# The order of the down projection's loads: from the planner's choice to program order, with two granules in other tiles

## The chip, the cores and the metric

The kernel runs on one core of a Trainium2 chip. The metric is the device time of one execution in microseconds; a profile is one further execution with the hardware profiler, with its own time beside its span. TensorE (PE) multiplies, VectorE (DVE), ScalarE (ACT) and GpSimd (POOL) work on tiles in SBUF, and transfers between DRAM and SBUF are issued here by SyncE (SP, plain loads and stores) and by POOL (among others the transfers that add into their target).

## The reference, cut to what matters

One layer of an encoder block is computed for two request groups of 256 and 512 tokens with the same weights, 768 tokens together: three token mixers side by side, a gated merge with an output projection and a residual, and then the feed-forward part, which ends in the product that this change touches:

```
D_MODEL = 1024
D_FF = 2816                      # -(-8 * D_MODEL // (3 * 256)) * 256

x = x + merged @ w_out[li]
h2 = rmsnorm(x, ffn_norm_g[li])
g, up = jnp.split(h2 @ w_gate_up[li], 2, axis=-1)
x = x + (jax.nn.silu(g) * up) @ w_down[li]      # (768 x 2816) @ (2816 x 1024)
```

Everything is float32. The two row groups of x are the outputs.

## The kernel before, in words

**Precision.** A float32 product is made of three matmuls on a high and a low part of each operand (`mm3`, lines 751 to 753). The parts come from a split: ACT rounds the operand into the high part (line 742 for weights, called `whd`, line 745 for hidden values, `dxh`), and DVE subtracts that from the operand (`wld`, line 743, and `dxl`, line 746).

**Gate and up.** The hidden dimension is worked through in 11 blocks `fb` of 256 columns, each a gate product and an up product (`block`). Each block's result stands in a tile `fa` (two in rotation, of 2 x 768 floats in each of 128 partitions) and is stored to DRAM as `hid_scr[fb]` by `hid_store` on SP (line 1425). The last steps of a block are products on POOL (line 1422). A block also uses two staging tiles of the pool `stg` (tag `brr`, 768 floats, two in rotation) for its sums; nothing uses them after the last block.

**Down.** The product of the hidden values (768 x 2816) with `w_down` (2816 x 1024) is cut into halves in all three dimensions and done with seven products in place of eight, in the order P2, P1, P5, P6, P3, P7, P4. The summed dimension is 2 x 1408, and each half is walked in six granules `g`: five of 256 and one of 128, the last being half of block 10. So there are 42 items (product, granule). An item multiplies a hidden granule (384 tokens) with a weight granule (512 columns): 3 token tiles x 2 slices x 3 matmuls = 18 matmuls with 512 columns, 9 for a half granule.

The hidden granules `da{r}{kh}_{g}` (r is the half of the tokens, kh that of the summed dimension) are loaded from `hid_scr` by `a_load` (line 1719), 384 KB each, 192 KB for the half one, 24 in all. P2 needs the six with (r, kh) = (0, 1), P1 the six with (0, 0), P5 the twelve with r = 1; the later products use sums of what is there. Granules 0 to 3 of P2 (blocks 5 to 8) have a pool of their own, `dae`. The other 20 have one tile each in the pool `downa`.

The weights come as quarters of 512 KB (256 KB for the half granule) by `w_fetch`: `dwr` tiles (P2, P3) into the weight stream's three raw buffers, `dwt` tiles (P7) into three buffers, and six `dch` tiles, which P1 loads (line 1737). P5, P6 and P4 each add another quarter to `dch` by an accumulating transfer from POOL (line 1747), after the tile's last split; P7 loads a `dwt` (line 1745) and adds a quarter to it likewise. `make` splits an item's weight and its hidden granule (or a sum of granules, line 1760). `item_loads` issues the hidden loads that an item is the first to need.

**Staging.** The main loop runs over the items; at item i it asks for the hidden loads of item i + 7 and the weights of item i + 6, splits item i + 2, and multiplies item i. Ahead of it, inside the last up block (`down_early`, a hook after that block's first product), the weights of items 0 to 2 and the hidden granules 0 to 3 of P2 are loaded and items 0 and 1 split. After the block, its store, and the closing of the pools of the feed-forward part, follow the hidden loads of items 4 to 6 and the weights of items 3 to 5. The high and low weight parts have four tiles each, the hidden parts three each. At the end of P1, P3, P7 and P4 the results are added to `x1` (line 1834) and stored (line 1836).

**Memory.** Pools lie on a stack. The pools of the down stage are opened after `XB` (the normalised input in two parts, 49,152 bytes in a partition) and the feed-forward pools behind it (first the two `fa` tiles, 12,288 bytes, then scratch, sums and factors) have been closed, and take their place from the same address: first `downa` (20 x 3,072 = 61,440 bytes, exactly XB and both fa tiles), then `dch` (six of 4,096), then the small ones.

**Order.** What each engine and each queue does is a fixed order, made when the program is built by a planner that follows a simulated timeline: of what is ready in its model it takes one after the other, so the order on SP, ACT or POOL need not be that of the program text. Waits keep it correct on the chip: an instruction waits for the data, and for the buffer, that it needs, and what stands behind it on its engine waits too. A call `tc.keep_in_program_order(ins)` adds an edge from the instruction traced last on the same engine to `ins`: it is queued behind it, without waiting for it to finish.

Of the kernel before, what the change touches and what calls it, by code (L numbers as in the profile page):

```python
# [8 lines left out]
F32 = mybir.dt.float32  # L9
# [617 lines left out]
def hybrid_block(ctx, tc, A, outs, consts):  # L627
    nc = tc.nc
    v, act, gp, pe = nc.vector, nc.scalar, nc.gpsimd, nc.tensor
    mul, add, sub = ALU.mult, ALU.add, ALU.subtract  # L630
# [200 lines left out]
    hid_scr = [dr.tile([128, 2, TOK], F32, name=f"hid_scr{fb}") for fb in range(NFB)]  # L831
# [139 lines left out]
    with tc.tile_pool(name="nrm", bufs=1) as pool, tc.tile_pool(name="nrmg", bufs=1) as pg:  # L971
# [43 lines left out]
        g = bcast_load(pg, A["norm_mix_g"][0], 1024, "gmix")  # L1015
# [107 lines left out]
    stg = x1ctx.enter_context(tc.tile_pool(name="stg", bufs=2))  # L1123
# [12 lines left out]
    for i, nme in enumerate(("diff_q_g", "diff_k_g")):  # L1136
        g = rp[:, 2, 64 * i : 64 * i + 64]
# [247 lines left out]
    with tc.tile_pool(name="gelu", bufs=1) as yp:  # L1385
        for m in range(2):
            gelu_load(m, yp)
        for j, h in enumerate(DIFF_HEADS):
# [3 lines left out]
            for n_v, u_ in enumerate(v_units(last // 2) if h is None else qk_units(h)):  # L1392
                n_unit += 1
                W.by_dma = n_unit >= LOADED and not final
                m, r = divmod(n_unit, GELU_UNITS)
# [4 lines left out]
                if final and n_v % 2:  # L1400

                    t = slice(128 * (n_v - 1), 128 * (n_v + 1))
# [8 lines left out]
    HT = TOK // 2  # L1411
# [68 lines left out]
    with ExitStack() as c5:  # L1480
# [66 lines left out]
        for c in range(4):  # L1547
            w = W.get()
            for m in range(2):
                M = 2 * c + m  # L1550
                t = gtp.tile([128, TOK], F32, name=uid("gt"), tag="glr")
# [151 lines left out]
    ITEMS = [(p, g) for p in range(7) for g in range(NG)]  # L1703
    AHEAD, FETCH, LOAD = 2, 6, 7
    EARLY = 4
    NEW = {P2: ((0, 1),), P1: ((0, 0),), P5: ((1, 0), (1, 1))}
    de = ctx.enter_context(ExitStack())
    de.enter_context(tc.tile_pool(name="dgap", bufs=1, side="right")).tile([128, 16], F32, name="dgap")
# [2 lines left out]
    DP, a_raw, ch, w_raw, parts = {}, {}, {}, {}, {}  # L1711

    def a_load(q, g):

        r, kh = q
        fb, m, n = granule(kh, g)
        early = q == (0, 1) and g < EARLY
        t = (da_e if early else DP["a"]).tile([128, 2, HT], F32, name=f"da{r}{kh}_{g}")[:, 0:n]
        nc.sync.dma_start(t, hid_scr[fb][:, m : m + n, HT * r : HT * r + HT])
        a_raw[q, g] = t  # L1720

    def w_quarter(kh, f, g):
        fb, m, n = granule(kh, g)
        return wd[:, 2 * fb + m : 2 * fb + m + n, 512 * f : 512 * f + 512]

    def w_fetch(i):

        if i >= len(ITEMS):
            return
        p, g = ITEMS[i]  # L1730
        n = granule(0, g)[2]
        view = lambda t: t.rearrange("p (k c) -> p k c", k=2)[:, 0:n]
        acc = None
        if p in (P1, P5, P6, P4):
            if p == P1:
                ch[g] = view(DP["ch"].tile([128, 1024], F32, name=f"dch{g}"))
                nc.sync.dma_start(ch[g], w_quarter(0, 0, g))
            else:
                acc = {P5: (0, 1), P6: (1, 1), P4: (1, 0)}[p]
            t = ch[g]  # L1740
        else:
            t = view(DP["r"].tile([128, 1024], F32, name=f"dwt{i}", tag="dwt") if p == P7 else
                     W.praw.tile([128, W.HALF], F32, name=f"dwr{i}", tag="wr"))
            src, acc = {P3: ((1, 1), None), P7: ((0, 1), (1, 1)), P2: ((1, 0), None)}[p]
            nc.sync.dma_start(t, w_quarter(*src, g))
        if acc:
            gp.dma_start(t, w_quarter(*acc, g), accum_op=add)
        w_raw[i] = t

    def make(i):  # L1750
# [39 lines left out]
    def down_early():  # L1790
        for i in range(3):
            w_fetch(i)
        for i in range(EARLY):
            item_loads(i)
        for i in range(AHEAD):
            make(i)

    for what, fb in order[2:]:
        block(what, fb, down_early if (what, fb) == order[-1] else None)
# [5 lines left out]
    with ExitStack() as c7:  # L1805
        for k, n in (("a", 1), ("ch", 1), ("t", 2), ("r", 3)):
            DP[k] = c7.enter_context(tc.tile_pool(name="down" + k, bufs=n))
        HOME = {P1: (0, 0, add), P5: (1, 1, add), P6: (0, 1, sub), P3: (0, 1, add), P7: (1, 1, sub),
                P2: (0, 0, add), P4: (1, 0, add)}
        acc = {}  # L1810
        for i in range(EARLY, LOAD):
            item_loads(i)
        for i in range(3, FETCH):
            w_fetch(i)
        for i, (p, g) in enumerate(ITEMS):
            item_loads(i + LOAD)
            w_fetch(i + FETCH)
            make(i + AHEAD)
            bank = "b" if p in (P1, P6, P7, P4) else "d"
            if g == 0 and p in (P1, P5, P2):  # L1820
                acc[bank] = [PS[bank].tile([128, 512], F32, name=uid("dn"), tag=bank) for _ in range(3)]
            ps = acc[bank]
            n = granule(0, g)[2]
            xh, xl, wh, wl = parts.pop(i)
            for t in range(3):
                c = slice(128 * t, 128 * t + 128)
                for k in range(n):
                    mm3(ps[t], xh[:, k, c], xl[:, k, c], wh[:, k], wl[:, k],
                        g == 0 and k == 0 and p in (P1, P5, P2), g == NG - 1 and k == n - 1, p in (P6, P3, P7, P4))
            if g == NG - 1:  # L1830
                r, f, op = HOME[p]
                for t in range(3):
                    o = x1[3 * r + t][:, 512 * f : 512 * f + 512]
                    v.tensor_tensor(out=o, in0=o, in1=ps[t], op=op)
                    if p in (P1, P3, P7, P4):
                        nc.sync.dma_start(os_[3 * r + t][:, 512 * f : 512 * f + 512], o)
# [45 lines left out]
```

## Time and profile before

| | us |
|---|---|
| time, median of 3 runs | 1786.07 (1783.4 to 1786.67) |
| the profiled execution's own time | 1785.03 |
| its span | 1783.3 |
| PE busy | 1746.8 (98%) |
| DVE busy | 1263.0 (71%) |
| ACT busy | 887.1 (50%) |
| POOL busy | 280.2 (16%) |
| first matmul of the down projection, from the start of the span | 1601.8 |
| start of its last matmul | 1778.8 |

The profile's page gives busy times and 40 slices of the span, with the clock that was granted to TensorE and the load on the DMA engines. A query of the trace narrows this to a stretch, a tile or an engine. An engine's instruction is written as line, engine, operation and "output <- inputs" by the names in the program, with tile numbers left out; "SPq" is the issue of a transfer, which lands later. In brackets, or behind a bar, stands the idle time ahead of it with what ended it.

### The profile page before, as it was taken

The page shows a single profiled execution, that of the slowest core. Times are in us where ns is not written, and L with a number is a line of the kernel's source. Part 1 is how long each engine was busy: PE and PEld are TensorE (multiplying, and loading weights), DVE is VectorE, ACT ScalarE, POOL GpSimd, SP SyncE. Part 2 cuts the span into 40 slices and gives each one's busy share as a digit, 9 for nine tenths or more (in the row PEclk, how much of TensorE's full clock was granted, in tenths as well). Part 3 has the DMA queues.
Part 4 walks back from the last instruction along what each step waited for, and adds up shares of the span by engine and source line. Part 5 has one row for each costly group of instructions (what it writes and reads, how often), then busy time and mean ns, then how long its engine had stood idle before and what let it go on. Part 6 is the DMA issues. An engine that isn't in the chain of part 4 may idle for free.

```text
span 1783.3 us, 29404 instructions
## 1 busy us (share of the span) xinstructions
PE 1746.8 (98%) x11194; PEld 1612.8 (90%) x11194; DVE 1263.0 (71%) x2342; ACT 887.1 (50%) x1856; POOL 280.2 (16%) x300
## 2 busy tenths in 40 slices
PE   9999999999999999999999999999999999997999
PEld 8999988999999999999978888888899999996787
DVE  6765659699999589778865535442797768764774
ACT  6445434777676356777755434232343334333343
POOL 0000000000000101110110002000136555532210
PEclk9999999999999999999999999999999999998999
DMA  7223745654656466453872437322223232349852
GB/s 255 82 84 97 141 112 127 165 144 132 154 144 153 125 160 157 113 113 78 179 174 78 135 116 248 115 93 83 71 78 107 89 115 98 125 144 320 163 115 67
DMA packets 209661, 234.09 MB, mean 131 GB/s; under 512 B 57832, under 2 KB 173296, under 8 KB 209520
## 3 DMA queue, kind: packets, MB, share of 16 engines
q1 hardware_dynamic: 184080, 164.05, 30.4%
q0 software_dynamic: 24288, 65.02, 17.1%
q10 hardware_dynamic: 1152, 3.15, 0.5%
q8 instruction: 88, 1.44, 0.3%
q14 instruction: 53, 0.43, 0.1%
HBM read 165.78 MB, written 41.22 MB: 116 GB/s over the span
## 4 chain that ended last, share of the span: by engine, by line
PE 56%; DMA 5%; DVE 1%; issue 1%; ACT 0%; POOL 0%; SPq 0%; DVEq 0%; ACTq 0%; POOLq 0%
PE br L752 4%; PE br L751 4%; PE br L753 4%; PE gate L751 3%; PE gate L752 3%; PE gate L753 3%; PE up L752 3%; PE up L751 3%; PE up L753 3%; DMA da<-hid_scr 2%; PE dn L753 2%; PE dn L752 2%; PE dn L751 2%; PE av L1311 2%; PE qk L752 2%; PE qk L751 2%
## 5 line engine op out<-in xcount | busy, mean ns | idle before, releaser
L595 ACT ACTIVATE wh<-wr 128x1024 fp32r<-128x1024 f32 x124 | 140.5, 1133 | 74.5 <-PE br L752 30.8
L601 DVE TENSOR_TENSOR wl<-wr,wh 128x1024 fp32r<-128x1024 f32 x82 | 108.3, 1323 | 84.8 <-ACT wh L595 83.0
L751 PE MATMUL gl<-Hhi,wh 128*128 128x256 f32 (+1 forms) x384 | 132.4, 345 | 2.3 <-ACT glt L1114 2.3
L753 PE MATMUL gl<-Hhi,wl 128*128 128x256 f32 (+1 forms) x384 | 129.0, 336 | 0.0
L752 PE MATMUL gl<-Hlo,wh 128*128 128x256 f32 (+1 forms) x384 | 128.7, 335 | 0.0
L751 PE MATMUL qk<-wh,Hhi 128*128 128x256 f32 x384 | 108.7, 283 | 0.6 <-ACT V L1210 0.6
L752 PE MATMUL qk<-wl,Hhi 128*128 128x256 f32 x384 | 109.3, 285 | 0.0
L753 PE MATMUL qk<-wh,Hlo 128*128 128x256 f32 x384 | 108.5, 282 | 0.0
L599 POOL DMA_DIRECT2D wl<-wr x42 | 36.6, 872 | 452.9 <-ACT wl L598 439.5
L751 PE MATMUL dn<-whd,dxh 128*128 128x512 f32 x231 | 91.8, 398 | 10.9 <-ACT dxh L745 10.9
L753 PE MATMUL dn<-whd,dxl 128*128 128x512 f32 x231 | 89.8, 398 | 3.6 <-DVE dxl L746 3.6
L752 PE MATMUL dn<-wld,dxh 128*128 128x512 f32 x231 | 91.6, 397 | 0.0
L751 PEld LDWEIGHTS gl<-Hhi,wh 128*128 128x128 f32 x384 | 72.3, 188 | 9.7 <-ACT glt L1114 2.7
L753 PEld LDWEIGHTS gl<-Hhi,wl 128*128 128x128 f32 x384 | 72.0, 188 | 8.0
L752 PEld LDWEIGHTS gl<-Hlo,wh 128*128 128x128 f32 x384 | 72.2, 188 | 7.2
L1280 DVE TENSOR_REDUCE nm<-sc 128x1 f32<-128x512 f32 (+1 forms) x96 | 56.6, 597 | 26.5 <-PE sc L1275 25.4
L751 PEld LDWEIGHTS qk<-wh,Hhi 128*128 128x128 f32 x384 | 73.1, 190 | 1.5 <-ACT V L1210 0.8
L753 PEld LDWEIGHTS qk<-wh,Hlo 128*128 128x128 f32 x384 | 73.4, 191 | 0.3
L752 PEld LDWEIGHTS qk<-wl,Hhi 128*128 128x128 f32 x384 | 73.1, 190 | 0.6
L745 ACT ACTIVATE dxh<-da 128x768 fp32r<-128x768 f32 (+1 forms) x36 | 28.5, 791 | 87.5 <-PE dn L752 58.3
L557 ACT ACTIVATE wh_S<-ws 128x512 fp32r<-128x512 f32 x70 | 41.2, 625 | 61.2 <-PE up L752 33.9
L558 DVE TENSOR_TENSOR wl_S<-ws,wh_S 128x512 fp32r<-128x512 f32 x70 | 58.4, 858 | 14.8 <-ACT wh_S L557 14.8
(478 smaller groups left out, 6039.4 us busy)
## 6 DMA issues: line engine op xcount, KB each, us to landing
wr<-in_w_in_dram SPq DMA_DIRECT2D x48, 512.0 KB, 4.8
wr<-in_w_gate_up_dram SPq DMA_DIRECT2D x44, 512.0 KB, 3.5
wl<-wr POOLq DMA_DIRECT2D x42, 512.0 KB, 5.2
wr<-in_w_branch_dram SPq DMA_DIRECT2D x24, 512.0 KB, 4.1
glr<-gl_scr POOLq DMA_DIRECT2D x24, 384.0 KB, 3.5
hid_scr<-fa SPq DMA_DIRECT2D x11, 768.0 KB, 6.4
wr<-in_w_mem_kv_dram SPq DMA_DIRECT2D x16, 512.0 KB, 3.7
wr<-in_w_in_dram SPq DMA_DIRECT2D x32, 256.0 KB, 4.3
```

Source lines behind the costliest of these rows:

```text
L557: self.nc.scalar.activation(f(hi), src, AF.Copy)
L558: self.nc.vector.tensor_tensor(out=f(lo), in0=src, in1=f(hi).bitcast(F32), op=ALU.subtract)
L595: self.nc.scalar.activation(hi, r, AF.Copy)
L599: self.nc.gpsimd.dma_start(lo, r.bitcast(F32R), accum_op=ALU.add)
L601: self.sub.tensor_tensor(out=lo, in0=r, in1=hi.bitcast(F32), op=ALU.subtract)
L745: act.activation(hi, src, AF.Copy, scale=scale)
L751: pe.matmul(ps, wh, xh, start=start, stop=False, **kw)
L752: pe.matmul(ps, wh, xl, start=False, stop=False, **kw)
L753: pe.matmul(ps, wl, xh, start=False, stop=stop, **kw)
L1280: v.tensor_reduce(out=nm[:, m : m + 1], in_=ps, axis=AX.X, op=ALU.max, negate=True)
L1311: pe.matmul(po[:, 0:128], aT[:, 128 * k : 128 * k + 128], V[:, c0 // 128 + k, 128 * (h % 2) : 128 * (h % 2) + 128], start=(k == 0), stop=( ...
```

## The change

All loads of hidden granules, all loads of down weights and all accumulating transfers are passed through `pin`, which is `tc.keep_in_program_order`. Granules 4 and 5 of the first product P2, so far the first two tiles of `downa`, go into the two staging tiles `brr`, and `downa` holds 18 tiles (55,296 bytes) in place of 20; the pools behind it begin 6,144 bytes lower. The weight loads of items 3 and 4 are asked for inside `down_early`, one behind each of its two splits, and so in the program text ahead of the last block's store; they were asked for after it. Item 5's stays where it was. The output stores and the hidden stores are not pinned, but a pinned load is queued behind those that stand ahead of it in the text.

```diff
@@
+    pin = tc.keep_in_program_order
@@ a_load
-        early = q == (0, 1) and g < EARLY
-        t = (da_e if early else DP["a"]).tile([128, 2, HT], F32, name=f"da{r}{kh}_{g}")[:, 0:n]
-        nc.sync.dma_start(t, hid_scr[fb][:, m : m + n, HT * r : HT * r + HT])
-        a_raw[q, g] = t
+        name = f"da{r}{kh}_{g}"
+        if q == (0, 1):
+            t = da_e.tile([128, 2, HT], F32, name=name) if g < 4 else \
+                stg.tile([128, 2, HT], F32, name=name, tag="brr")
+        else:
+            t = DP["a"].tile([128, 2, HT], F32, name=name)
+        a_raw[q, g] = t[:, 0:n]
+        pin(nc.sync.dma_start(t[:, 0:n], hid_scr[fb][:, m : m + n, HT * r : HT * r + HT]))
@@ w_fetch
-                nc.sync.dma_start(ch[g], w_quarter(0, 0, g))
+                pin(nc.sync.dma_start(ch[g], w_quarter(0, 0, g)))
...
-            nc.sync.dma_start(t, w_quarter(*src, g))
+            pin(nc.sync.dma_start(t, w_quarter(*src, g)))
         if acc:
-            gp.dma_start(t, w_quarter(*acc, g), accum_op=add)
+            pin(gp.dma_start(t, w_quarter(*acc, g), accum_op=add))
@@ down_early
         for i in range(AHEAD):
             make(i)
+            w_fetch(i + 3)
@@
-        for i in range(3, FETCH):
+        for i in range(AHEAD + 3, FETCH):
             w_fetch(i)
```

## The prediction

> **What bounds the kernel now.** I began with the page: where TensorE stops, and at what clock it goes on.
>
> ```profile
> span 1783.3 us, 29404 instructions
> PEclk9999999999999999999999999999999999998999
> ```
>
> A slice is 44.6 us; the one dip of the granted clock is the 37th, 1605 to 1650, inside the down projection, which is the stretch that the diff touches. The next view is a table of stages for the instructions of its accumulator tile alone, then the same tile's list with first and last start, then what PE waited for.
>
> ```profile
> 1601.80:1618.30 16.50, 16.48 (x72) 13.36 (x72) 0.00 (x0) 1.00 1.05 375
> 1618.30:1629.20 10.90, 0.05 (x1) 0.00 (x1) 0.00 (x0) 0.60 1.11 253
> 1629.20:1634.30 5.10, 5.10 (x13) 3.99 (x14) 0.00 (x0) 0.53 1.10 248
> 1634.30:1658.60 24.30, 24.30 (x108) 19.89 (x106) 1.96 (x3) 1.00 1.09 312
> 1662.40:1668.20 5.80, 5.80 (x14) 4.54 (x15) 0.68 (x1) 0.50 0.42 70
> 1668.20:1779.20 111.00, 110.94 (x490) 91.51 (x488) 10.92 (x17) 1.00 0.50 106
> ```
>
> ```profile
> L751 PE MATMUL dn<-whd,dxh x231: 387/389/792, 1601.8 to 1778.3; 128*128 128x512 f32 x116
> L753 PE MATMUL dn<-whd,dxl x231: 388/389/792, 1602.3 to 1778.8; 128*128 128x512 f32 x116
> ```
>
> ```profile
> PE dn L751 <- ACT dxh L745: 10.9, 1, 10.9
> PE dn L753 <- DVE dxl L746: 3.6, 1, 3.6
> ```
>
> In a stage row the first pair is PE's busy time and count, and the last three figures are the granted clock, the DMA share and GB/s. PE stops twice, 10.9 and 3.6 us, and after each stop runs some 13 matmuls at half clock (0.53, 0.50). At full clock a matmul takes 110.94 / 490 = 0.2264 us. From the first start to the last (1778.8 - 1601.8 = 177.0 us) lie 692 steps of the 693 matmuls (three forms of 231), which need 156.7 us. **So 20.3 us are lost here**: 14.5 in the two waits, 5.10 - 13 x 0.2264 = 2.2 and 5.80 - 14 x 0.2264 = 2.6 in the slow clock behind them, the other 1.0 at the modelled edges. The 490 matmuls from 1668 on have no hole.
>
> What PE waited for are splits of hidden granules, and these waited for loads. The SP queue in order of time, then three pieces of the chain that ended last:
>
> ```profile
> 1591.71 4.53 SPq L1745 DMA_DIRECT2D dwr<-in_w_down_dram  x2
> 1597.86 2.99 SPq L1737 DMA_DIRECT2D dch<-in_w_down_dram  x6
> 1600.88 0.53 SPq L1745 DMA_DIRECT2D dwt<-in_w_down_dram  x1
> 1601.51 0.49 SPq L1745 DMA_DIRECT2D dwr<-in_w_down_dram  x1
> 1602.34 1.69 SPq L1745 DMA_DIRECT2D dwt<-in_w_down_dram  x2
> 1605.05 0.34 SPq L1425 DMA_DIRECT2D hid_scr<-fa  x1
> 1606.40 5.97 SPq L1745 DMA_DIRECT2D dwr<-in_w_down_dram  x3
> 1615.07 30.11 SPq L1719 DMA_DIRECT2D da<-hid_scr  x20
> ```
>
> ```profile
> 1605.05 9.94 DMA hid_scr<-fa
> 1616.94 20.02 DMA da<-hid_scr
> 1644.85 16.33 DMA da<-hid_scr
> ```
>
> Product P2, the first, uses six dwr tiles, and P7, the sixth, the dwt tiles. So three dwt loads (P7) and the three dwr loads at 1606.40 (the seventh to ninth, of P3, the fifth product) went out ahead of the hidden granules that P2 and P1, the next products, still lacked. All 20 of those sit in a pool over the memory of XB and of the two fa tiles (20 x 3,072 = 49,152 + 12,288 bytes), and the first was issued at 1615.07, when the last fa tile's store had landed (1605.05 + 9.94). They then joined a queue that was already full: 20.0 and 16.3 us to landing.
>
> **The change, part by part.** With no stall, a full granule (18 matmuls) takes 4.08 us and the half one 2.04; P2 starts at 1601.8, its items 4 and 5 at 1618.1 and 1622.2, P1 at 1624.2, P5 at 1646.6, and the last pair of P5 at 1667.0.
>
> *Right granules 0 to 3 of P2 move behind three weight loads.* They were issued one by one, the first at 1466.9; pinned, they follow the third dwr load, and the first two dwr loads follow the store of block 9.
>
> ```profile
> L1719 SPq DMA_DIRECT2D da<-hid_scr x24: 326/544/5322, 1466.9 to 1644.8; - x24
> 1574.73 1.79 SPq L1745 DMA_DIRECT2D dwr<-in_w_down_dram  x2
> 1576.98 0.34 SPq L1425 DMA_DIRECT2D hid_scr<-fa  x1
> 1587.38 4.70 SPq L1745 DMA_DIRECT2D dwr<-in_w_down_dram  x2
> da<-hid_scr SPq DMA_DIRECT2D x1, 384.0 KB, 3.4
> 1580.00:1600.00 20.00, 20.00 (x117) 20.00 (x116) 12.24 (x20) 7.34 (x11) 3.55 (x3) 1.00 0.41 136
> L745 ACT ACTIVATE dxh<-da 128x768 fp32r<-128x768 f32 x27 | 22.8, 844 | 63.2 <-PE dn L752 48.7 <-DMA da<-hid_scr 12.1 <-PE dn L753 2.4
> L746 DVE SCALAR_TENSOR_TENSOR dxl<-da,dxh 128x768 fp32r<-128x768 f32 x27 | 25.7, 953 | 26.7 <-ACT dxh L745 26.7
> ```
>
> The two dwr loads lose under 3 us, and splitting them begins later anyway (the slots for halves come free as PE leaves the block). The four loads (4 x 0.54 us of SP) go out at about 1587.8 to 1590. Alone one takes 3.4 us; with the dwr load 2.1 MB are under way, 5.8 us at 0.36 MB/us, so they land between 1591.5 and 1594. Three granules are then split inside the last block, at 0.84 us of ACT and 0.95 of DVE each, 2.5 and 2.9 us; cover is there (ACT 7.3, DVE 12.2 of 20 us busy), and the first is needed at 1601.8. Cost: 0; without the cover, at most these 5.4 us.
>
> *The fourth and fifth dwr load move ahead of the last store in the program text.* Their buffers, and so their times (1591.71 and 1595.9), stay as they are. 0.
>
> *The store is alone.* Nothing is left on SP between 1596.3 and the store. Its last product on POOL ends at 1603.72, so it starts 1.3 us sooner, and with only granule 4's load beside it (now in a staging tile, free with that same product) takes between the 4.6 us of one alone and the 9.94 of this one; I take 6.5, nearer the lower, as the queue is empty. It lands at 1610.3 (1608.4 to 1613.7).
>
> ```profile
> 1601.72 2.00 POOL L1422 TENSOR_TENSOR fa<-fa,fs 128x384 f32<-128x384 f32 x2 [1.62 <-DVE fs L1458]
> hid_scr<-fa SPq DMA_DIRECT2D x1, 768.0 KB, 4.6
> da<-hid_scr SPq DMA_DIRECT2D x4, 384.0 KB, 18.7
> dch<-in_w_down_dram POOLq DMA_DIRECT2D x1, 512.0 KB, 15.8
> L742 ACT ACTIVATE whd<-dch 128x1024 fp32r<-128x1024 f32 x20 | 20.9, 1045 | 6.1 <-PE dn L753 6.1
> L743 DVE TENSOR_TENSOR wld<-dch,whd 128x1024 fp32r<-128x1024 f32 x20 | 24.4, 1219 | 6.3 <-ACT whd L742 6.3
> ```
>
> *Everything else of SP queues behind granule 5, which waits for that store.* This is the added wait: behind it stand P2's last dwr (256 KB) and, in turn, a hidden granule and a dch tile for each item of P1, none of which needs the store, and which before were half there (dch out at 1597.86). Rates: plain loads moved 375 GB/s before the stall, the mixes 248 to 312; I count 0.36 and, as a bound, 0.25 MB/us. From 1610.3, up to the first dch go 0.20 + 0.39 + 0.26 + 0.39 + 0.52 = 1.77 MB, 4.9 to 7.1 us and 2.3 to land (3.4 us of the load alone less its 1.1 at that rate): 1617.5 to 1620. P1's first split must begin 2.3 us (1.05 + 1.22) ahead of 1624.2, at 1621.9. Each further item brings 0.92 MB, 2.5 to 3.7 us of 4.08. Granule 4 lands by 1610, 8 us early, granule 5 and the last dwr by 1615, 7 us early. Cost: 0; each us by which the store is later than 1613 would show in PE from here on.
>
> *P5's pairs.* After P1's 5.5 MB (done by 1626 to 1632) come six pairs of hidden granules, 4.3 MB, and beside them on POOL six accumulating transfers, 2.9 MB, that start as before when P1's weights are split. 7.2 MB take 23 us at 0.31 and 29 at 0.25: 1649 to 1661. The last pair is needed 3 us ahead of 1667.0, at 1664. Cost: 0, with a margin of 3 us at the bound.
>
> *Loads and transfers that move later.* P3's dwr loads go behind P1's output stores (1649), 40 us early for a product that starts near 1691. P7's first three dwt go behind P3's last dwr, that is behind the split of P3's third weight.
>
> ```profile
> 1704.19 9.96 SPq L1745 DMA_DIRECT2D dwr<-in_w_down_dram  x3
> dwt<-in_w_down_dram POOLq DMA_DIRECT2D x1, 512.0 KB, 7.5
> 1740.78 0.90 POOL L1747 DMA_DIRECT2D dwt<-in_w_down_dram  x1 [3.36 <-DVE wld L743]
> ```
>
> The last of those three went out at 1713.8, 2 us after P3's start (1779.1 - 3 x 22.4 = 1711.9). So the first dwt goes out 2.5 us into P3, lands 3.7 later, and its sum (7.5) is there at 14 us of P3's 22.4; it is split near 20. P4's transfers now stand on POOL behind P7's last, which goes out 6.5 us into P7 (1740.8 against 1779.1 - 2 x 22.4 = 1734.3): the first lands at 15 and is split at 20. Cost 0, margins 5 to 6 us. Removed with them: 4.7 MB (three dwr, three dwt and their sums) from the queue of 1601 to 1629.
>
> **The sum**: -20.3 us, nothing set against it. The profiled execution took 1785.03 us, 1.7 over its span, and the median of the three runs is 1786.07. 1785.0 - 20.3 = 1764.7; on the median, **1765.8, which I round to 1766**.
>
> **The rivals.** *A, the first wait stays in part.* ACT works in a fixed order, and in the old one it converts a hidden granule behind weights of later items. If granule 4's conversion stands behind the first or second split of P1's dch (1617 to 1620) it ends 3 us after 1618.1, plus 2.4 for the clock: **1771**. Against it: granule 4 no longer lands after them, so the planner has no reason for that order.
>
> *B, the second wait stays.* POOL's transfers do not wait their turn with SP: a dch sum issued at 1617 took 15.8 us beside hidden loads that took 18.7. If SP gets half of 0.36 MB/us as long as sums run (from 1619.5), its 9.8 MB less 3.3 end at 1656; with half of the 0.31 of the mixes, at 1662; a little less, and the old 3.6 + 2.6 us are back: **1772**. The Trainium skill, DMA: Bandwidth & Descriptors, section Queues, rings and completion order, states that each DMA engine goes round-robin between the queue rows that have work, a packet at a time; by that rule program order on SP gives its loads no precedence over POOL's, and the time would be B's 1772 rather than 1766.
>
> *C, slower: the wait for the store starves SP.* Between 1615 and 1661 SP's 7.1 MB moved at only 0.15 MB/us. If its 9.8 MB behind the store run no faster, the last pair lands at 1610 + 65 = 1675, 12 us late, and with two cold clocks (4.8) most is given back: **1783**. It decides below 0.135 (73 us, 19 us late, +24 with the clock): **1790**. Against it: in those 46 us 5 to 6 MB of other traffic ran beside SP, now 2.9.
>
> *D, the planner's new order undoes it.* Pins also move what ACT and DVE do in between; both partial waits together would leave **1778**.
>
> **How the numbers follow.** Full recovery 0.56, A 0.15, B 0.13, D 0.05, C 0.11 (0.03 of it within 0.2%, 0.08 slower). 0.2%, 3.6 us, is about what a measurement of this kernel tells from no change. Faster 0.88, same 0.04, slower 0.08. The range for 8 in 10 takes in full recovery, A and B with some play: 1763 to 1776.
>
> **What would show it.** Right: one row of hidden loads after the store without dwt or early dwr between; landings of 4 to 10 us instead of 13 to 20; no PE wait over 1 us between 1601 and the end and no row under clock 1.00; last matmul near 1758.5. Wrong: ACT waiting on a dwr or dch load ahead of granule 4 (A); DVE's subtraction on a load after 1645 (B); SP idle past 1613 for the store (C); P2 starting later than 1602 (the moved granules).

## The result, and the profile after

| | before | after |
|---|---|---|
| median of 5 runs each | 1786.07 us (1783.4 to 1787.73) | 1779.35 us (1776.34 to 1780.47) |
| ratio, 95% interval | | 0.9962 (0.9948 to 0.9977) |
| profiled execution, span | 1785.03, 1783.3 us | 1780.2, 1778.4 us |
| down projection, first matmul's start to the last one's end | 1601.82 to 1779.14: 177.32 us | 1606.17 to 1774.30: 168.13 us |

The change makes the kernel faster by 4.1 to 9.3 us (0.23% to 0.52% of 1786), 6.7 in the medians. The prediction said 20 us, and the time lies above its range. In the two profiled executions the stage is 9.2 us shorter, of which 4.4 are missing from the whole because the stage started later; what that is comes below.

The same table of stages as before, for the instructions of the accumulator tile alone, of the kernel after. The columns are PE's busy time (matmuls), weight loads, DVE, then the granted clock, the DMA share and GB/s.

```profile
1606.18:1641.28 35.10, 35.10 (x154) 28.72 (x154) 2.04 (x3) 1.00 0.89 267
1641.28:1644.63 3.35, 0.01 (x1) 0.00 (x0) 0.00 (x0) 1.00 1.06 390
1644.63:1645.13 0.50, 0.49 (x1) 0.19 (x1) 0.00 (x0) 0.91 1.10 384
1645.13:1647.07 1.94, 0.00 (x1) 0.01 (x1) 0.00 (x0) 0.50 1.06 373
1647.07:1652.20 5.13, 5.13 (x13) 4.08 (x14) 0.00 (x0) 0.53 1.10 290
...
1749.54:1751.59 2.05, 0.00 (x0) 0.03 (x1) 0.68 (x1) 1.00 1.13 206
```

And what PE waited for in that stage, in us, times, and the longest:

```profile
PE dn L752 <- DVE wld L743: 3.3, 1, 3.3
PE dn L751 <- DVE x L1840: 2.0, 1, 2.0
PE dn L753 <- DVE dxl L746: 1.9, 1, 1.9
```

The wait of 10.85 us inside P2, ahead of its fifth granule, is gone: 154 matmuls, P2 and half of P1, run in one piece at full clock. But two new waits stand in P1, 35 us into the stage, 3.35 and 1.94 us; the clock falls in between, and 13 matmuls then take 5.13 us instead of 2.94, 2.2 us too many. A third, of 2.05 us, stands at the start of P4, the last product. With the one slow matmul between the first two (0.3) that is 9.8 us; the stage is 10.85 longer than the 157.28 us that it takes without a hole (shown below), and the remaining 1.0 us is spread over the edges of these stretches.

The SP queue, in order of time:

```profile
1596.07 6.24 SPq L1750 DMA_DIRECT2D dwr<-in_w_down_dram  x2
1607.60 0.53 SPq L1725 DMA_DIRECT2D da<-hid_scr  x1
1609.55 0.34 SPq L1425 DMA_DIRECT2D hid_scr<-fa  x1
1613.21 0.96 SPq L1725 DMA_DIRECT2D da<-hid_scr  x2
...
1624.46 1.90 SPq L1725 DMA_DIRECT2D da<-hid_scr  x2
```

The pins did what they say: granule 4, the store, then granule 5 and everything else in program order, and no weight of P3 or P7 in between. The two loads at 1624.46 are the first pair of P5. The second of them, issued at 1625.83, landed at 1642.39, 16.6 us later. DVE, in order:

```profile
1631.93 0.95 DVE L746 SCALAR_TENSOR_TENSOR dxl<-da,dxh 128x768 fp32r<-128x768 f32 x1
1642.48 0.96 DVE L1765 TENSOR_TENSOR da<-da,da 128x768 f32<-128x768 f32 x1 [9.60 <-DMA da<-hid_scr]
1643.36 1.22 DVE L743 TENSOR_TENSOR wld<-dch,whd 128x1024 fp32r<-128x1024 f32 x1
1645.19 0.96 DVE L1765 TENSOR_TENSOR da<-da,da 128x768 f32<-128x768 f32 x1 [0.61 <-DMA da<-hid_scr]
1646.06 0.95 DVE L746 SCALAR_TENSOR_TENSOR dxl<-da,dxh 128x768 fp32r<-128x768 f32 x1
```

DVE stood 9.60 us before the subtraction of that pair (L1765), and behind it in its fixed order stood the split of P1's fourth weight (L743 at 1643.36), for which PE stopped at 1641.28; the second pair's subtraction stood in the same way ahead of that item's other low part, the hidden granule's (L746 at 1646.06). The pair belongs to P5, which PE reached only at about 1659 (44.8 us into the stage, as the prediction has it, and 7.8 lost): P1 waited for a product that comes after it.

### The profile page after: what moved, and what is told of

Same layout as the page of the kernel before. It is cut to its first block, busy times and chain, and to the rows that moved or that the text cites. A ratio compares the mean times of both kernels' runs of the same rounds, so it can differ in the third digit from the quotient of the medians.

```text
span 1778.4 us, 29418 instructions
## 1 busy us (share of the span) xinstructions
PE 1747.6 (98%) x11194; PEld 1613.2 (91%) x11194; DVE 1265.1 (71%) x2342; ACT 888.0 (50%) x1856; POOL 282.2 (16%) x300
## 3 DMA queue, kind: packets, MB, share of 16 engines
HBM read 165.78 MB, written 41.22 MB: 116 GB/s over the span
## 4 chain that ended last, share of the span: by engine, by line
PE 55%; DMA 4%; DVE 2%; issue 1%; SPq 1%; ACT 0%; POOL 0%; ACTq 0%; DVEq 0%; POOLq 0%
PE br L751 4%; PE br L752 4%; PE br L753 4%; PE gate L751 3%; PE gate L753 3%; PE up L753 3%; PE gate L752 3%; PE up L752 3%; PE up L751 3%; PE dn L753 2%; PE dn L751 2%; PE dn L752 2%; PE av L1311 2%; PE qk L752 2%; PE qk L751 2%; PE qk L753 2%
## 5 line engine op out<-in xcount | busy, mean ns | idle before, releaser
L751 PE MATMUL gl<-Hhi,wh 128*128 128x256 f32 (+1 forms) x384 | 132.4, 345 | 2.3 <-ACT glt L1114 2.3
L751 PE MATMUL qk<-wh,Hhi 128*128 128x256 f32 x384 | 108.8, 283 | 0.4 <-ACT V L1210 0.4
L751 PE MATMUL dn<-whd,dxh 128*128 128x512 f32 x231 | 90.7, 393 | 2.0 <-DVE x L1840 2.0
L751 PEld LDWEIGHTS gl<-Hhi,wh 128*128 128x128 f32 x384 | 72.3, 188 | 9.7 <-ACT glt L1114 2.7
L751 PEld LDWEIGHTS qk<-wh,Hhi 128*128 128x128 f32 x384 | 73.1, 190 | 1.5 <-ACT V L1210 0.6
L1282 ACT ACTIVATE p<-sc,nm 128x512 f32<-128x512 f32 (+1 forms) x96 | 59.1, 620 | 17.5 <-DVE nm L1280 17.0
```

The lines of the kernel that those rows point to most:

```text
L751: pe.matmul(ps, wh, xh, start=start, stop=False, **kw)
L1282: act.activation(pm[:, 0:n], ps, AF.Exp, bias=nm[:, m : m + 1], accum_out=s1s[:, tt : tt + 1] if m == 0 else s2)
```

## The experiments

The first theory was this order on DVE; the rival was that the loads are too slow, whoever waits for them. A second question was why the pair took 16.6 us, a third the wait in P4, a fourth which half of the change does the work. In the table "stage" is from the first dn matmul's start to the last one's end in the profiled execution; it takes 692 x 0.2264 = 156.7 us from start to start, and 157.28 to the end, when nothing is in the way.

| run | stage, us | PE waits over 1 us | median, us | ratio to before (95%) |
|---|---|---|---|---|
| before | 177.32, again 175.63 | 10.85, 3.64; again 11.95, 2.19 | 1786 to 1787 | 1 |
| staging tiles alone | 178.24 | 2.93, 3.48, 6.18 | 1789.51 | 1.0013 (1.0002 to 1.0024) |
| pins alone | 171.77 | 1.22, 3.44, 1.41, 2.73 | 1778.68 | 0.9957 (0.9943 to 0.9971) |
| after | 168.13, again 168.35 | 3.35, 1.94, 2.05; again 2.20, 2.55, 2.13 | 1779.35 | 0.9962 (0.9948 to 0.9977) |
| after, transfers free | 165.78 | 3.33, 1.63 | 1776.85 | 0.9941 (0.9924 to 0.9958) |
| after, subtraction pinned | 163.94 | 1.73, 2.04 | 1773.37 | 0.9926 (0.991 to 0.9943) |
| after, both | 160.23 | 2.65 | 1775.63 | 0.9931 (0.9914 to 0.9948) |
| after, loads ahead | 161.31 | 1.93, 1.42 | 1774.38 | 0.9936 (0.992 to 0.9953) |
| after, loads ahead, subtraction pinned | 157.28 | none | 1769.23 | 0.9903 (0.989 to 0.9917) |
| after, all three | 157.28, again 157.28 | none | 1764.28, again 1767.99 | 0.9879 (0.9859 to 0.9898), again 0.9893 (0.9877 to 0.991) |
| after, without P5's sums | 157.31 | none | 1770.87 | 0.9915 (0.989 to 0.994) |

**The subtraction in program order.** One pin in make(), so that a pair's subtraction can't go ahead of the splits of P1 that the program names first:

```
-            tt(x, x, A_(1, 1), sub)
+            pin(tt(x, x, A_(1, 1), sub))
```

> The changed kernel with one more pin: the subtraction that forms P5's left operand (line 1765) stays behind the weight split of its own item on DVE. Theory 1 (the wait left in P1 and P5 comes from DVE's fixed order, in which the first P5 pair's subtraction stands ahead of the weight split of P1's fourth item and holds it until the pair has landed at 1642.4): the two PE waits of 3.35 and 1.94 us and the slow clock behind them go, 8 us of the 168.1 us between the first and the last matmul of the down projection, which becomes 160, and the time 1771; the 2 us wait ahead of P4 stays. Rival 2 (the loads themselves are too slow, whoever waits for them): PE waits as long on a later item, 166 to 169 us, time within 2 us of the changed kernel.

DVE's first subtraction of a pair now comes at 1646.85, after the splits. PE's waits in this run:

```profile
PE dn L751 <- DVE x L1840: 2.0, 1, 2.0
PE dn L753 <- DVE dxl L746: 2.0, 2, 1.7
...
```

The two waits of 3.35 and 1.94 us are gone, and no stretch is below full clock. So the order was the cause of these two. But the loads are just as late, and small waits come in their place, now in P5: 0.37, 0.26, 0.52 and 1.73 us between 1648 and 1662. The stage is 163.9 us, between the 160 of the theory and the 166 of the rival: the order made the lateness dear, it did not make it.

**The accumulating transfers free.** The pin of POOL's transfers alone taken back:

```
-            pin(gp.dma_start(t, w_quarter(*acc, g), accum_op=add))
+            gp.dma_start(t, w_quarter(*acc, g), accum_op=add)
```

> The changed kernel with the accumulating transfers not pinned; the loads stay pinned. The planner then puts P4's six transfers ahead of P7's on POOL, as in the kernel before. Theory 1 (the 2.05 us PE wait ahead of P4 comes from P4's first sums landing late behind P7's, which holds the weight splits and, behind these on DVE, the adds that P4's first matmuls need): that wait goes, 2 us less, 166 of 168.1 us in the down projection, time about 2 us under the changed kernel; the waits of P1 and P5 stay at 3.4 and 1.9. Rival 2 (P4's wait is only the end of P7 on DVE, as the order of the adds has it): no difference.

The wait at P4's start (PE dn L751 <- DVE x) is gone and the other two are there as before: 2.4 us less of stage, 2.5 less in the medians, where the two intervals overlap. Of after, the chain of work that ended last shows how that wait came about:

```profile
1729.09 7.71 DMA dwt<-in_w_down_dram
1737.38 0.90 POOL dwt L1752
1738.66 9.78 DMA dch<-in_w_down_dram
...
1749.62 1.23 DVE wld L743
```

P4's six transfers stand on POOL behind the last sum of P7, which waits for its load; that load took 7.71 us and landed at 1736.8. The second sum of P4 landed at 1748.4, ACT and DVE split it, and behind the split on DVE stood the adds of P7's output (x, L1840), which free the accumulator that P4 starts on.

**Both edits.**

> Both edits together: P5's subtraction pinned on DVE, the accumulating transfers not pinned. Theory 1 expects the sum of both gains, 10 us: no PE wait over 1 us in the down projection, 157 to 158 us between its first and last matmul, time about 1769. Rival 2 (late loads): 165 us or more, time over 1775.

The accumulator tile by stages in this run, one row of it, and DVE at the same place:

```profile
...
1660.51:1663.16 2.65, 0.00 (x1) 0.00 (x0) 0.00 (x0) 1.00 1.11 297
...
```

```profile
1660.41 1.83 DVE L1765 TENSOR_TENSOR da<-da,da 128x768 f32<-128x768 f32 x2 [1.46 <-DMA da<-hid_scr]
```

One wait of 2.65 us is left, the stage is 2 to 3 us longer than expected, and the wait is P5's own: a pair that landed at 1660.3, when PE wanted its granule at 1660.5. This time nothing stands in a wrong order. The loads are late, and the next run asks why. The medians don't follow here: with a stage 3.7 us shorter than the subtraction alone the run is 2.3 us slower, inside the scatter of both (1771.56 to 1776.53 and 1770.82 to 1777.22).

**P5's accumulating transfers left out.**

```
-        if acc:
+        if acc and p != P5:
```

> The changed kernel without the accumulating transfers of P5 (the second quarter of w_down is not added to the weights that P5 multiplies; this part of the result is left out). The order of every engine stays. Theory 1, the accumulating transfers on POOL (issued at 1625, 1629, 1631 and on) take part of what moves while SP's loads of hidden granules are under way: in the changed kernel 7.6 MB moved in the 29 us from 1613.2 to 1642.4, 0.26 MB/us, 1.6 MB of it sums. Without them SP's 6.0 MB move at the 0.36 MB/us of plain loads, 17 us, and the first pair of P5 lands at about 1632 instead of 1642.4; the two PE waits of 3.35 and 1.94 us and the cold clock behind them go, the down stage takes 161 instead of 168.1 us, and the time is about 1772. Rival, SP's loads are limited by themselves (issue cadence, buffers that come free late): the pair lands at 1639 to 1642, at least one wait of 2 to 3 us stays, the stage takes 166 to 168 us and the time is 1777 to 1779.

The DMA share and GB/s from 1600 to 1660 in slices of 1.5 us, with the queues (packets, MB, share of 16 engines), of after:

```profile
DMA  5082008924978999999999999999999999999405
GB/s 207 12 239 102 0 3 279 394 111 117 256 228 300 357 399 376 400 388 379 382 259 248 259 248 250 254 247 311 398 383 373 374 359 230 211 217 196 91 15 79
...
q1 hardware_dynamic: 7165, 11.85, 57.3%
q0 software_dynamic: 1562, 3.00, 27.5%
```

and of the run without P5's sums, from 1600 to 1650 in slices of 1.25 us:

```profile
DMA  0580007980689979999999999999999950000038
GB/s 10 75 324 20 0 0 198 392 354 0 168 187 329 273 267 342 406 384 403 385 379 388 374 379 376 376 374 372 375 374 374 371 198 32 0 0 20 0 34 151
...
q1 hardware_dynamic: 6999, 11.55, 67.1%
```

In both the 16 engines are full (9). Without the sums they move 371 to 388 GB/s from 1624 to 1640; with them 250, from the 21st slice on (1630), for 10 us. The first pair landed at 1632.89, 28.0 us into the stage instead of 36.2, within a microsecond of the 1632 expected, and with the same order on DVE PE waited for nothing; the stage takes 157.3 us where 161 was expected. DVE at that pair, and the accumulator tile over the whole stage:

```profile
1632.98 0.96 DVE L1765 TENSOR_TENSOR da<-da,da 128x768 f32<-128x768 f32 x1 [1.82 <-DMA da<-hid_scr]
```

```profile
1604.92:1762.24 157.32, 157.31 (x693) 129.89 (x693) 13.60 (x20) 1.00 0.67 177
```

So the sums on POOL take the room of SP's loads, and more of it than their bytes say. From the queue rows of after: plain loads 0.573 x 60 us / 11.85 MB = 2.9 us of all 16 engines for a MB, sums 0.275 x 60 / 3.00 = 5.5. The same in the window 1600 to 1660 of before:

```profile
q1 hardware_dynamic: 8280, 14.02, 66.3%
q0 software_dynamic: 2317, 4.45, 40.1%
```

2.8 and 5.4. A sum costs 1.9 times a plain load of its size. What had to land up to the first pair in after (6.03 MB of loads, 1.57 MB of sums, from 1613.2) takes 6.03 x 2.9 + 1.57 x 5.5 = 26.1 of the 29.2 us up to 1642.4. In the same time 1.0 MB of loads moved that go out behind the pair; with these it is 29.1.

That adding is dear, and not POOL's queue, is seen earlier in the trace of after, where this queue carries a plain load: from 985.4 to 991.5 one of 0.39 MB took 20.8% of the 16 engines, 0.208 x 6.1 / 0.39 = 3.3 us for a MB, and SP's loads beside it 0.451 x 6.1 / 0.94 = 2.9.

The Trainium skill, Collectives: The Full Stack, section The bandwidth ceiling: the fold count and why AG ≠ RS ≠ AR, puts the halving of an adding transfer's rate (1.93 there) down to its reading two sources; it is measured on a ring of four ranks. The 1.9 here agrees with the ratio; the reason no run here shows. The Trainium skill, DMA: Bandwidth & Descriptors, section Queues, rings and completion order, has the round between queue rows that the prediction held against the change. The runs agree with what it would do here: order on SP gave SP's loads no precedence over POOL's sums (the pair at 36.2 us with them, 28.0 without).

**Staging tiles alone**, on the kernel before, without a pin.

```
-        early = q == (0, 1) and g < EARLY
-        t = (da_e if early else DP["a"]).tile([128, 2, HT], F32, name=f"da{r}{kh}_{g}")[:, 0:n]
+        name = f"da{r}{kh}_{g}"
+        if q == (0, 1):
+            t = da_e.tile([128, 2, HT], F32, name=name) if g < EARLY else \
+                stg.tile([128, 2, HT], F32, name=name, tag="brr")
+        else:
+            t = DP["a"].tile([128, 2, HT], F32, name=name)
+        t = t[:, 0:n]
         nc.sync.dma_start(t, hid_scr[fb][:, m : m + n, HT * r : HT * r + HT])
```

> The kernel before with one part of the change alone: granules 4 and 5 of P2 in the staging tiles, nothing pinned, no load asked for earlier. The planner then still issues P7's first three and two of P3's weight loads ahead of granule 5. Theory 1 (the gain came from clearing the queue of P3's and P7's loads): little, within 3 us of before, and PE still waits 6 to 11 us near P2's fifth and sixth item. Rival 2 (the gain came from the two granules no longer waiting for the pool): most of the 9 us that the down projection gained, and the first PE wait gone.

What PE waited for in this run:

```profile
PE dn L752 <- DVE wld L743: 6.5, 2, 6.2
PE dn L753 <- DVE dxl L746: 4.1, 2, 3.5
PE dn L751 <- ACT whd L742: 2.9, 1, 2.9
...
```

The first wait falls from 10.85 to 0.5 us, since granule 4 no longer waits for the store; the 6 to 11 us expected near P2's fifth and sixth granule did not come. But three loads of P7 and two more dwr loads still go out ahead of granule 5, and PE now stops twice in P1 (2.93 us at its first weight, 3.48 at its last low part) and once in P5 (6.18). Nothing is gained.

**Pins alone**, with the earlier weight requests: granules 4 and 5 stay in the pool over the fa tiles.

```
-            t = da_e.tile([128, 2, HT], F32, name=name) if g < 4 else \
-                stg.tile([128, 2, HT], F32, name=name, tag="brr")
+            t = (da_e if g < 4 else DP["a"]).tile([128, 2, HT], F32, name=name)
```

> The pins without the two staging tiles: left granules 4 and 5 of the first product lie in the pool of the others, over the memory of the fa tiles, so both are loaded only when the last store has landed (1613.2 in the changed kernel). Theory, the program order of the loads is what removes the first wait, and the staging tiles bring little: granule 4 goes out at about 1613.2 beside granule 5, lands by 1617 to 1619, where P2 needs its split at about 1622.5 (16.3 us after its start); no wait of PE before 1640 over 1 us, the down stage 168 to 170 us, the time 1779 to 1781. Rival, the staging tiles are needed: granule 4 lands after 1621, PE waits 2 us or more for it and loses clock, the down stage takes 172 us or more, the time is 1783 or more.

The SP queue of this run when the store had landed:

```profile
1612.97 1.75 SPq L1724 DMA_DIRECT2D da<-hid_scr  x3
```

Granule 4 went out with granule 5, landed at 1616.6, and PE did not wait for it. What follows are waits of the kind that after has, at P1's fourth and fifth granule and at P4, a little longer, and a stage of 171.8 us, 2 more than expected. This profile is of the slowest of ten executions (1783.69 us), and the median can't be told from after's. The pins, with the requests moved ahead, carry the gain.

**Loads ahead of the store.** In after SP has nothing to send from 1602.3 to 1607.6 and from 1609.9 to 1613.2 except one granule. This edit asks for three dch loads and P2's last dwr load there, and lays the pool of dch tiles so that it is free of the fa tiles:

```
-        for k, n in (("a", 1), ("ch", 1), ("t", 2), ("r", 3)):
+        for k, n in (("a", 1), ("t", 2), ("ch", 1), ("r", 3)):
...
+        for i in range(FETCH, FETCH + 3):
+            w_fetch(i)
+        for i in range(AHEAD + 3, FETCH):
+            w_fetch(i)
         for i in range(EARLY, LOAD):
             item_loads(i)
-        for i in range(AHEAD + 3, FETCH):
-            w_fetch(i)
...
-            w_fetch(i + FETCH)
+            if i > 2:
+                w_fetch(i + FETCH)
```

First with the other two edits (subtraction pinned, transfers free):

> The changed kernel with the subtraction of P5's pairs in program order and the accumulating transfers free (as in the run of both), and three dch loads and the last dwr load of P2 asked for ahead of the store, in the stretch 1602 to 1607 in which SP had nothing to do; the pool of dch tiles changes places with that of the later hidden loads, so that it no longer lies over the fa tiles. With both edits alone the down stage took 160.2 us with one wait of 2.65 us left, for a pair that landed at 1660.3. Theory, that pair came late because SP's loads behind the store share a rate of about 0.26 MB/us with the sums: 1.8 MB moved ahead of the store bring the pair 5 to 7 us sooner, the wait goes, the down stage takes 157.5 to 158.5 us, and the time is 1770 to 1773. Rival, the loads ahead of the store delay the store (3.6 us alone) to 8 us or more, and everything behind it with it: a wait of 1 to 3 us stays and the time is as with both edits, 1775.

The SP queue of this run around the store, and the accumulator tile over the whole stage:

```profile
1596.70 1.46 SPq L1742 DMA_DIRECT2D dch<-in_w_down_dram  x3
...
1603.91 0.34 SPq L1425 DMA_DIRECT2D hid_scr<-fa  x1
1607.70 3.58 SPq L1725 DMA_DIRECT2D da<-hid_scr  x6
```

```profile
1600.67:1757.96 157.29, 157.28 (x693) 129.88 (x693) 13.45 (x20) 1.00 0.77 193
```

All 693 matmuls in 157.29 us at full clock, the first pair landed 25.2 us into the stage, and the store, with loads ahead of it, still took 3.7 us. The stage can't be shorter for this number of matmuls at 0.2264 us each, and the time, 1764.28 us, is some 6 us below what was expected. This beats both kernels. Then the same edit without the other two:

> The changed kernel with only the loads ahead of the store (three dch loads and P2's last dwr load asked for in SP's idle stretch, the pools of dch and of the later hidden loads exchanged); the subtraction of P5's pairs is free again and the accumulating transfers stay pinned. With all three edits the down stage took 157.3 us, the first pair of P5 landed 25 us after the stage's start instead of 36, and no wait was left. Theory, DVE's order (the pair's subtraction ahead of the split of P1's fourth weight) costs only what the pair is late; the pair then lands at about 25 us, DVE reaches its subtraction at about 27 us, and the two waits at P1's end go without touching the order; the wait of 2 us in P4 stays, as P4's transfers still stand behind P7's. Down stage 158 to 160 us, time 1765 to 1768. Rival, the order itself costs: later pairs, or the sums, keep splits of P1 waiting, at least one PE wait of 2 us or more before 60 us of the stage, stage 162 to 166 us, time 1769 to 1774.

DVE in this run, in order of time:

```profile
1631.71 0.96 DVE L1765 TENSOR_TENSOR da<-da,da 128x768 f32<-128x768 f32 x1 [7.42 <-DMA da<-hid_scr]
...
1633.18 0.95 DVE L746 SCALAR_TENSOR_TENSOR dxl<-da,dxh 128x768 fp32r<-128x768 f32 x1
```

The pair is 9 us earlier, but the order written out for DVE has moved its subtraction forward as well, ahead of P1's second low part, and DVE again stood 7.42 us. PE waited 1.93 us there and 1.42 in P4. This is nearer the rival: the early landing alone doesn't disarm the order. And with the loads ahead and the subtraction pinned, but the transfers pinned too:

> The loads ahead of the store and the subtraction of P5's pairs in program order, with the accumulating transfers pinned as in the changed kernel: it differs from the run of all three edits (157.3 us of down stage, 1764.3 us) only in these pins. Theory, the pins of the accumulating transfers cost the wait in P4 and nothing else: one PE wait of about 2 us there, down stage 159 to 160 us, time 1766 to 1767. Rival, the wait in P4 came from the lateness of what stood before it (loads of P5 that held up the sums): no wait, 157 to 158 us, 1764 to 1765.

The accumulator tile over the whole stage in this run:

```profile
1605.09:1762.38 157.29, 157.28 (x693) 129.89 (x693) 13.44 (x20) 1.00 0.76 194
```

No wait in P4, though POOL has after's order there. So the theory that the pin as such costs the 2 us falls, and the rival holds: the place behind P7's last sum costs only when that sum is late. The load before it, of 256 KB, took 4.8 us here and 7.7 in after, and P4's transfers went out 120.3 us into the stage; in after it was 131.8, of which 8.8 are PE's earlier losses. The remaining 2.7 us are the difference between no wait and 2.05.

**The same kernels again.** Of after, of before, and of the version with all three edits:

> The changed kernel once more, for a second profile. If the 4.4 us by which its down projection started later (1606.18 against 1601.80) are the chance of one execution, the start moves by some us while the down stage takes 168 us within 1, with the same two waits at P1's end and the one in P4. If they belong to the change, the start is again at 1606 within 0.5.

> The kernel before once more, for a second profile. If the start of its down projection (1601.80) is the chance of one execution, it moves within the 1600.7 to 1606.2 seen in the other profiles, while the stage takes 177 us within 1 and the waits of 10.9 and 3.6 us stay; if the early start belongs to this kernel, it is again at 1602 within 0.5.

> All three edits once more (loads ahead of the store, subtraction in program order, accumulating transfers free): the first time 157.3 us of down stage and 1764.3 us, 5 us less than the run without the last edit, whose stage is as long (157.3 us, start at 1605.10 against 1600.67). If these 5 us are chance of the executions ahead of the stage, the stage takes 157.3 us again, its start lies anywhere in 1600.7 to 1606.2, and the median comes out between 1764 and 1770; if the early start belongs to this kernel, the start is at 1601 within 1 and the median at 1764 to 1766.

The start of the stage moved each time, to 1603.33 (after), 1605.33 (before) and 1604.90 (all three), while the length hardly did for after and all three (168.35 and 157.28 us); that of before fell by 1.7 us to 175.63, more than the 1 us expected, with waits of 11.95 and 2.19 us. In 14 profiles the starts lie between 1600.67 and 1606.18 and do not go with the kernel. So the 4.4 us by which after's stage began later are chance of the executions; so are most of the 5 us between 1764.3 and 1769.2 of the two versions whose stages are equal.

## Why the prediction was wrong, point by point

**Held.** The reading of what bounds the stage, 20.3 us lost to two waits and the clock, is right: three kernels without these losses (one of them leaves out P5's sums) have a stage of 157.3 us, 20.0 less than before, and take 1764 to 1771, where the forecast for full recovery was 1766. The moved granules cost 0, as said: their sign, P2 starting later than 1602, was there (1606.18), but the start scatters in before as well (1601.8 and 1605.3), and from 1590 on PE waited for nothing ahead of it. The store was alone, but did not start 1.3 us sooner: 3.4 us into the stage, in before 3.2. It took 3.6 us where 6.5 were forecast and landed at 1613.15, 7.0 us into the stage; forecast were 8.5, and before had 13.2. Granule 4, granule 5 and P1's first weights came in time, and the first wait, 10.85 us and its cold clock, is gone. P3's and P7's later loads harmed nothing of P3 and P7.

**Where it failed: the step "P5's pairs ... Cost: 0, with a margin of 3 us at the bound".** What failed is the deadline. It was taken from the product that uses the pairs, 1664 for the last. But DVE's order, in before as in after, puts the first pair's subtraction ahead of the split of P1's fourth weight, so the pair is wanted where PE needs that split, 35 us into the stage, less the 2.15 us from the subtraction's start to PE: 33 us in. P5 begins at 44.8 (1646.6 - 1601.8). The first pair landed 36.2 us in; the price was 5.3 us of waits and 2.5 of clock. The subtraction that waited for the last load of the pairs started at 1658.30, so this load landed some 52 us in, within the forecast (1649 to 1661, which is 47 to 59) and in time for its own use.

The trace of before held this order, and its price too. Of before, DVE in order of time:

```profile
1642.82 0.96 DVE L1760 TENSOR_TENSOR da<-da,da 128x768 f32<-128x768 f32 x1 [0.99 <-DMA da<-hid_scr]
1643.69 0.95 DVE L746 SCALAR_TENSOR_TENSOR dxl<-da,dxh 128x768 fp32r<-128x768 f32 x1
1644.56 1.22 DVE L743 TENSOR_TENSOR wld<-dch,whd 128x1024 fp32r<-128x1024 f32 x1
...
1658.93 0.96 DVE L1760 TENSOR_TENSOR da<-da,da 128x768 f32<-128x768 f32 x1 [4.67 <-DMA da<-hid_scr]
1661.27 0.56 DVE L1760 TENSOR_TENSOR da<-da,da 128x384 f32<-128x384 f32 x1 [1.38 <-DMA da<-hid_scr]
1661.74 0.55 DVE L746 SCALAR_TENSOR_TENSOR dxl<-da,dxh 128x384 fp32r<-128x384 f32 x1
```

The first pair came in time for P1's fourth weight there, as P1 had itself been held up by the first wait. But all six pairs stand ahead of the low part of P1's last granule (L746 at 1661.74), and for the last two DVE waited 4.67 and 1.38 us. The granule itself was there long before: ACT had begun its high part at 1649.91. So the second wait of before, 3.64 us, was already P1 waiting for P5's pairs; the prediction read it as a split that waited for a load, and did not ask for whose. Removing the first wait moved the demand for the first pair forward by 11 us and left the order.

The price of the mixture was off by less. While the sums ran the core moved 0.25 MB/us, the step's bound and not its 0.31, and not by bad luck but since a sum takes 1.9 times its bytes. With 2.8 and 5.4 us a MB from before's queues, the step's own 4.3 MB of pairs and 2.9 MB of sums come to 27.7 us, near the long end of its 23 to 29. Lateness and order made the two waits together: the run without P5's sums took away the lateness and the run with the subtraction pinned the order, and either removes them. And the step set only the last pair against its use: with the subtraction pinned and the transfers free, the one wait left, 2.65 us, was for P5's third granule.

**The second failure: P4's transfers behind P7's, "Cost 0, margins 5 to 6 us".** It cost 2.05 us. The margin was reckoned for the first of P4's sums alone, and that one's split came as forecast, 19 us into P7. But they go out six in a row, and DVE's adds of the output stand behind the second's split. It is a consequence of lateness further up: with the same pins and earlier loads the cost was 0.

**The rivals.** B, that POOL's transfers share with SP whatever the order on SP, is the right mechanism for the lateness, as the run without P5's sums shows; its mark, a subtraction on DVE after 1645, was 1642.5 and 1645.2 here, with the whole stage 4.4 us later. Its price of 6.2 us was near the 7.8 measured in P1, but that is luck: it reckoned with the deadline of P5's own use and left out P4. A did not happen: ACT's conversions were in time. C's mark, SP idle past 1613 for the store, was there for 0.2 us, and the pairs were not starved as it has it. D names what did happen in general, the planner's order; but it wasn't new: pinned loads left DVE's old order in force, and the order was wrong for the new times. That its 1778 lies near the 1779.35 is luck too: it adds A's wait, which did not come, to B's.

**The rest.** 20.0 - 10.85 = 9.2 us of stage against 6.7 in the medians (interval 4.1 to 9.3); with the second profiles 8.2 as the mean of both. That rest is within what the starts of the stage scatter by.

## What to carry to other kernels

Take the deadline of a load not from the instruction that uses its data but from the first instruction queued behind that one on the same engine: with orders written out in advance, a subtraction for the next product can stop this one. Price a mixture of transfers by the engines' time and not by bytes: the queue rows of the profile give the share of the 16 engines and the MB for each queue, and here an adding transfer cost 1.9 times a plain one. And when a pin puts loads behind a slow event, look for idle time of that queue ahead of the event: 1.8 MB sent there, with one more pin on DVE, recovered the 20 us of stage of which the change alone got 9.

## What the runs showed of the hardware

A sum occupies the DMA engines 1.9 times as long as a load of its size (5.4 to 5.5 against 2.8 to 2.9 us for a MB on all 16; a plain load on POOL's queue 3.3), and the whole core falls from 375 to 250 GB/s while sums run. SP sends no further load while some seven are under way: from 1622 on nearly each went out 0.02 us after an earlier one had landed, as in this piece of after's chain, where a load landed at 1632.28:

```profile
1621.11 11.17 DMA da<-hid_scr
1632.30 6.55 SPq L1725
```

Whether the program or the chip sets that number was not tried. And the clock: PE waits of 1.93, 2.05 and 2.65 us left it at 1.00, but in the second profile of before one of 2.19 us did not (the accumulator tile by stages, the granted clock third from the end):

```profile
1663.08:1665.27 2.19, 0.00 (x2) 0.00 (x1) 0.00 (x0) 1.00 0.06 16
1665.27:1670.00 4.73, 4.73 (x14) 3.74 (x15) 0.00 (x0) 0.64 0.30 38
```

The clock records of the traces show what decides. In all 14 profiles the granted clock changes only in steps of 3.41 us (at half clock it stays for 3.41, 6.83 or 13.65 us). Of the steps of the down stage that began at full clock, each that had no matmul in 60% or more of its time was followed by half clock (eleven, 0.60 to 0.96), and none of the 644 others, with 51% or less, was. The 2.19 us lay within one step, which had no matmul in 64% of its time; the 2.65 us were divided between two, 45% and 33%. So a wait of 2 to 3 us can go either way, by how it falls on the steps.

The Trainium skill, TensorE: Matmul & The Clock Gate, section Part 1: The HAM clock gate (the "warmup" mystery), has the clock fall after an idle window of about 3.4 us that runs free of the kernel. The length and the free running agree with these records; that the window must be idle throughout they do not show, since 60% was enough.
